# Latent and forgetting attention: value products one unit later, two token blocks at a time

## The chip, the cores and the metric

The kernel runs on 1 core of one Trainium2 chip. The metric is the device time of one launch in microseconds (us). Engines carry the names of the profile: PE is the tensor engine's matmul, PEld its weight load, DVE the vector engine, ACT the scalar engine, POOL GpSimd, SP the engine that issues most DMAs.

## The reference

The program computes one transformer block with two kinds of attention, and then two layers of a second kind with a convolution branch, a gated short convolution and latent attention. 512 tokens, width 1024, float32. What the change touches are two of the attentions. The first block's forgetting attention (8 heads of 64, after 16 meta tokens), for a block of 128 queries:

```python
sb = jnp.einsum('bqhd,bkhd->bhqk', q_blk, k) * scale
sb = sb + c_blk[..., None] - cum[:, :, None, :]
sb = jnp.where(k_pos[None, :] <= q_pos[:, None], sb, NEG_INF)
pb = jax.nn.softmax(sb, axis=-1).astype(v.dtype)
return jnp.einsum('bhqk,bkhd->bqhd', pb, v)
```

and the latent attention of the two later layers (8 heads, queries and keys of 64 + 32, values of 64), for a block of 128 queries:

```python
s = jnp.einsum("bqhd,bkhd->bhqk", qb, k) * scale
s = jnp.where(mask[None, None], s, -jnp.inf)
p = jax.nn.softmax(s, axis=-1).astype(v.dtype)
return jnp.einsum("bhqk,bkhd->bqhd", p, v)
```

Both are causal over the 512 tokens. The results go through output projections; everything else (norms, projections, feed-forward, convolutions, gates) is untouched.

## The kernel before

Activations are kept feature-major as [128, 512 tokens] tiles, each split in two float32r parts (hi, lo), so that a projection is three matmuls of 512 columns per 128 inputs (`mm3`, L117 to L122). A projection of one [128, 512] output is 24 such matmuls.

Both attentions work in units (i, b): pair of heads i (0 to 3), query block b (0 to 3), 16 units per attention; the latent attention runs once in each of two layers. A unit has two stages. `first` makes the scores of the two heads (tiles `s`: L687 and L690 in `fox`, L1531 to L1534 in `mla`), reduces them on DVE, takes exp on ACT into `L`, and scales `L` on DVE. `second`, one unit behind, transposes the b + 1 blocks of `L` of each head on PE into a PSUM tile (`pT`, L720 and L1554), copies that to SBUF on ACT (`ptile`, L722 and L1556), and multiplies it by the values into the PSUM tile `pv` (L726 and L1560): 2(b + 1) products with a stationary operand of 128 x 64, one head in each half of `pv`. At b = 3 the pair is closed: `fox` adds the meta tokens' product (L729) and splits `pv` (`mix_split`), `mla` gates it on DVE (`om`, L1564) and splits it. The scores and the transposes share three PSUM banks (`spp`), `pv` is a single bank (`pvp`), and the SBUF tiles for `pT` are two (`tp`).

Between the units stand fillers: projections (`pj`, `qn`, `qr`, `kb`, `q`), and in the later half of `fox` steps of the output projection (`y`). In `mla` they are spread by `pipeline` (L207), in `fox` by a table of steps. In `mla` the convolution's taps (L1217) run on DVE meanwhile.

The order on each engine isn't the order of the code: a scheduler places the instructions by priority (earlier code first) and by its own estimate of when their inputs are ready, so that matmuls of a filler stand between a unit's transposes and its value products. On the chip each engine runs its instructions in the order thus fixed.

Of the kernel before, what the change touches and what calls it, by code (L numbers as in the profile page):

```python
# [19 lines left out]
P = 128  # L20
# [18 lines left out]
class Cols:  # L39
    """[128, 8, 128] in two parts"""  # L40
# [8 lines left out]
class Kern:  # L49
    def __init__(self, ctx, tc, t, out):  # L50
        self.tc, self.nc, self.t, self.out = tc, tc.nc, t, out
        ep = lambda **k: ctx.enter_context(tc.tile_pool(**k))
        self.const = ep(name="const", bufs=1)
        self.wp = ep(name="wp", bufs=3)
        self.rowp = ep(name="rowp", bufs=3)
        self.ap = ep(name="ap", bufs=57)
        self.lp = ep(name="lp", bufs=3)
        self.tp = ep(name="tp", bufs=2)
        self.fp = ep(name="fp", bufs=4)
        self.qp = ep(name="qp", bufs=2)  # L60
        self.smp = ep(name="smp", bufs=32)
        self.mmp = ep(name="mmp", bufs=4, space=PSUM)
        self.spp = ep(name="spp", bufs=3, space=PSUM)
        self.pvp = ep(name="pvp", bufs=1, space=PSUM)
        self.dram = ep(name="dram", bufs=1, space=DRAM)
        self.n = 0
        self.bg = []
        self.rate = 0
        self.ahead = AHEAD
        self.lat_w = []  # L70
# [65 lines left out]
    def wrows(self, src):  # L136
        """a [128, 1024] row block, kept: hi and lo as two slabs each"""
# [15 lines left out]
    def wcols(self, w, c0, n, kt=KD):  # L153
        """[K, cols] -> hi, lo views [128, kt, n]"""
# [6 lines left out]
    def wkeep(self, w, c0):  # L161
        """[1024, 128] columns in slabs of their own"""
# [3 lines left out]
    def split(self, hi, lo, src, scale=None):  # L166
        """hi, lo <- src (SBUF or PSUM), optionally times a constant"""
# [8 lines left out]
    def rsqrt(self, v, n):  # L176
        """1 / sqrt(v), polished by a Newton step"""
# [19 lines left out]
    def bcast_row(self, dst, src, parts=P, eng=None):  # L197
        """DRAM row [n] -> all partitions"""
# [8 lines left out]
    def pipeline(self, first, second, fillers, lead=1):  # L207
        """units of two stages, the second one behind by some units; other work spread between them"""
        n, credit, fillers = len(first), 0.0, list(fillers)
        rate = len(fillers) / (n + lead)  # L210
        for i in range(n + lead):
            if i < n:
                first[i]()
            if i >= lead:
                second[i - lead]()
            credit += rate
# [7 lines left out]
    def setup(self):  # L224
        """everything small that the start needs, behind the first rows of x"""
# [43 lines left out]
    def squares(self, src, a, b, dve=False):  # L269
        """a, b <- row sums of squares of the halves of src [., 1024]"""  # L270
# [9 lines left out]
    def sumsq(self, rows):  # L280
        """[128, len(rows)] row sums of squares"""
# [38 lines left out]
    def warm(self, n):  # L320
        """keeps the tensor engine busy, so that its clock is up when the first products come"""
# [18 lines left out]
    def meta_rep(self):  # L340
        nc = self.nc
        mhi, mlo = self.mhl
        # replicated 8 times: [128, k, 8, 16]
# [10 lines left out]
    def swa_bias(self):  # L354
        """negated T5 bias with the window mask, per head: [meta | prev | cur] and, for the first block, [meta | cur]"""
# [41 lines left out]
    def q_load(self, i):  # L397
        """tile i holds heads i and i + 4"""
# [7 lines left out]
    def swa_first(self):  # L406
        """keys of the first half of the tokens, as soon as these are there"""
# [45 lines left out]
    def proj_v(self):  # L453
        """v_a, v_b and f, token-major"""
# [14 lines left out]
        # column halves: [v_a 128 | v_b 0:196] and [v_b 196:512 | f 8]  # L469
# [67 lines left out]
    def forget_sums(self):  # L537
        nc, ls = self.nc, self.ls
        # inclusive sums over the tokens, [head, token]
# [18 lines left out]
    def forget_rows(self, i):  # L558
        """the sums of two heads on all partitions"""
# [14 lines left out]
    def fox_k(self, i):  # L574
        """two steps, a half of the tokens each"""
# [17 lines left out]
    def probs(self, Lg, mn, den):  # L593
        """exp(min - Lg) in place, its sum in den"""
# [72 lines left out]
    def fox(self, mix, fillers):  # L667
        """pairs of heads one after another; fillers: a list per step"""
# [35 lines left out]
        def second(i, b):  # L704
            if b == 0:
                st[i, "pv"] = self.pvs()
            pv, Lt = st[i, "pv"], st.pop((i, b))
            n = (b + 1) * P
            tk = slice(b * P, n)
# [6 lines left out]
            pT = []  # L716
# [6 lines left out]
            for j in range(b + 1):  # L723
                for half in range(2):
                    h = 2 * i + half
                    nc.tensor.matmul(pv[64 * half:64 * half + 64, tk], lhsT=self.vb[j][:, h * 64:(h + 1) * 64],  # L726
                                     rhs=pT[half][:, j * P:(j + 1) * P], start=(b == 0), stop=False)
            if b == NB - 1:
                nc.tensor.matmul(pv, lhsT=self.vmF[:32, i * P:(i + 1) * P], rhs=pmT, start=False, stop=True)  # L729
# [3 lines left out]
        for s in range(len(u) + 1):  # L733
            if s < len(u):
                first(*u[s])
            if s:
                second(*u[s - 1])
            for f in fillers.get(s, ()):
                f()

    def tokmm(self, acts, wrow, kt, blocks, post, banks, tail=0):
        """token-major product as a list of steps: acts(k, b) -> (hi, lo) [128, 128 tokens]; wrow(k) -> hi, lo [2][128, 512];
        in the last `tail` row blocks the token blocks follow one another"""
# [42 lines left out]
    def add_rms(self, xs, g, ps):  # L786
        """x += rms_norm([p0 p1]) * g for some row tiles"""
# [10 lines left out]
    def to_feat(self, rows, hi, lo, c0, scale, bank, bias=None):  # L798
        """token-major row tiles -> feature-major hi, lo [k][:, c0:...], scaled and shifted per feature"""
# [208 lines left out]
    def layer_consts(self, l):  # L1008
        """per-channel vectors of a layer as columns"""
# [28 lines left out]
    def ada(self, l):  # L1038
        """queue the modulation of a layer: shift, 1 + scale as feature columns, gate as a row in DRAM"""
# [16 lines left out]
        def total(third):  # L1056
            """sums over the partitions, as a row in DRAM"""
# [31 lines left out]
    def colsum(self, ps, c0, src):  # L1089
        """ps[:, c0 + b] <- sums over the partitions of src[:, token block b]"""  # L1090
# [3 lines left out]
    def allsum(self, src):  # L1094
        """sums over the partitions [128, 512] in PSUM, the same in each partition"""
# [7 lines left out]
    def spread(self, cols, d):  # L1103
        """per-token columns [128, 4] -> [128, 512] in PSUM, the same in each partition; d: a tile to work in"""
# [33 lines left out]
    def layer_begin(self, l, u, banks):  # L1138
        """the part that needs the first half of the tokens only"""
# [7 lines left out]
    def layer(self, l, finish, xd):  # L1147
# [5 lines left out]
        # latents  # L1153
# [40 lines left out]
        # branch A input, in the shadow of the latents' norms  # L1194
# [28 lines left out]
        # values and keys  # L1223
# [31 lines left out]
        # attention and branch B  # L1255
# [4 lines left out]
        def uq(i):  # L1260
            """queries of two heads; the rotary rows of four heads come together: [odd 3 | odd 1 | even 0 | even 2] by 32"""
# [73 lines left out]
        # merge  # L1335
# [25 lines left out]
        # branch A: layer norm in the shadow of the gates  # L1361
# [53 lines left out]
        # merge of branch A, w_o  # L1415
# [76 lines left out]
    def nope(self, ps):  # L1492
        """two heads' rows -> the even head's tile [nope | rope | -] and the odd one's [0 | rope | nope]"""
# [9 lines left out]
    def rope_parts(self, ps, n):  # L1503
        """two tiles whose sum is the rotated rows"""
# [13 lines left out]
    def mla(self, Q, K, V, cg, oc, fillers):  # L1518
# [25 lines left out]
        def second(i, b):  # L1544
            n = (b + 1) * P
            tk = slice(b * P, n)
            if b == 0:
                st[i] = self.pvs()
            pv, Lt = st[i], st.pop((i, b))
            pT = []  # L1550
# [6 lines left out]
            for j in range(b + 1):  # L1557
                for half in range(2):
                    h = 2 * i + half
                    nc.tensor.matmul(pv[64 * half:64 * half + 64, tk], lhsT=V[j][:, h * 64:(h + 1) * 64],  # L1560
                                     rhs=pT[half][:, j * P:(j + 1) * P], start=(b == 0), stop=(b == NB - 1 and j == b))
            if b == NB - 1:
# [9 lines left out]
        self.pipeline([lambda a=a: first(*a) for a in u], [lambda a=a: second(*a) for a in u], fillers)  # L1572
# [90 lines left out]
```

## Time and profile before

| | |
|---|---|
| three runs | 1796.34 us median (1795.69 to 1797.44) |
| span of the profiled execution | 1792.5 us |
| PE busy | 1745.6 us (97%) |
| DVE busy | 1142.4 us (64%) |
| ACT busy | 690.2 us (39%) |
| forgetting attention (L687 to L729) | about 157 to 275 us |
| latent attention, first and second layer | about 800 to 955 us, about 1350 to 1505 us |

Busy time of PE counts each matmul from its start to a modelled end, and neighbours overlap, so 97% doesn't say that PE gets through its work as fast as it could. Better is the distance from one start to the next in the timeline. A float32 matmul such as the value product is two instructions on PE: 80 products on L726 and 160 on L1560 are 160 and 320 rows in the trace. The transposes and the float32r matmuls are one each.

### The profile page before, as it was taken

What the parts mean: (1) busy time and instruction counts of PE and PEld (TensorE: products, weight loads), DVE (VectorE), ACT (ScalarE), POOL (GpSimd) and SP (SyncE); (2) the same over time, 40 slices, a digit from 0 to 9 for tenths busy, and PEclk for the clock granted to TensorE, in tenths of its full rate; (3) what the DMA queues carried; (4) which work ended last, traced back from release to release, by engine and by line L of the source; (5) the groups of instructions that cost most, each with busy time, mean ns of one, the idle gap of its engine ahead of it and who ended that gap; (6) DMA issues with size and microseconds to landing.
All of it is one profiled execution on the core that took longest, in us unless ns stands there. A gap on an engine that the chain in (4) does not pass through costs nothing.

```text
span 1792.5 us, 22688 instructions
## 1 busy us (share of the span) xinstructions
PE 1745.6 (97%) x8652; PEld 1390.8 (78%) x8652; DVE 1142.4 (64%) x1963; ACT 690.2 (39%) x1294; POOL 53.4 (3%) x110
## 2 busy tenths in 40 slices
PE   6999999999999999999999999998999999999997
PEld 6877767877778879877777888877877777888876
DVE  5354457865833464579786584468479796774657
ACT  4454455333333455354432223333444443222430
POOL 2000001000000000100000000000100000000000
PEclk9999999999999999999999999999999999999999
DMA  4412136575833574422223333335232223333332
GB/s 130 117 48 82 48 95 223 193 246 161 277 121 130 189 245 139 101 77 68 64 71 94 94 94 94 94 105 174 83 84 68 64 71 86 100 85 106 87 101 94
DMA packets 263479, 206.39 MB, mean 115 GB/s; under 512 B 43924, under 2 KB 239800, under 8 KB 263370
## 3 DMA queue, kind: packets, MB, share of 16 engines
q1 hardware_dynamic: 263082, 204.67, 38.9%
q8 instruction: 68, 1.11, 0.3%
q14 instruction: 41, 0.34, 0.1%
q10 hardware_dynamic: 288, 0.26, 0.1%
HBM read 196.48 MB, written 8.43 MB: 114 GB/s over the span
## 4 chain that ended last, share of the span: by engine, by line
PE 88%; DVE 6%; ACT 2%; issue 2%; DMA 2%; POOL 0%; SPq 0%; DVEq 0%; ACTq 0%; POOLq 0%
PE pj L120 11%; PE pj L122 11%; PE pj L121 11%; PE gu L121 4%; PE gu L122 4%; PE gu L120 4%; PE y L751 3%; PE y L752 3%; PE y L753 3%; PE yt L122 2%; PE yt L121 2%; PE yt L120 2%; PE pv L1560 2%; PE lat L122 1%; PE lat L120 1%
## 5 line engine op out<-in xcount | busy, mean ns | idle before, releaser
L132 ACT CAST whi<-raw 128x1024 fp32r<-128x1024 f32 (+4 forms) x275 | 283.6, 1034 | 761.8 <-PE pj L121 377.9
L133 DVE TENSOR_TENSOR wlo<-raw,whi 128x1024 fp32r<-128x1024 f32 (+4 forms) x275 | 330.3, 1203 | 304.0 <-ACT whi L132 302.0
L120 PE MATMUL pj<-uh,whi 128*128 128x512 f32 x896 | 357.4, 399 | 0.0
L121 PE MATMUL pj<-ul,whi 128*128 128x512 f32 x896 | 355.2, 396 | 0.0
L122 PE MATMUL pj<-uh,wlo 128*128 128x512 f32 x896 | 355.2, 396 | 0.0
L122 PEld LDWEIGHTS pj<-uh,wlo 128*128 128x128 f32 x896 | 168.4, 188 | 40.3 <-issue 3.4
L120 PEld LDWEIGHTS pj<-uh,whi 128*128 128x128 f32 x896 | 168.8, 188 | 38.9 <-issue 3.1
L121 PEld LDWEIGHTS pj<-ul,whi 128*128 128x128 f32 x896 | 168.8, 188 | 38.3 <-issue 2.6
L1217 DVE SCALAR_TENSOR_TENSOR conv<-apad,lcol,conv 128x512 f32<-128x512 f32 x240 | 179.6, 748 | 4.8
L122 PE MATMUL gu<-h2h,wlo 128*128 128x512 f32 x320 | 126.2, 395 | 0.0
L121 PE MATMUL gu<-h2l,whi 128*128 128x512 f32 x320 | 126.2, 394 | 0.0
L120 PE MATMUL gu<-h2h,whi 128*128 128x512 f32 x320 | 126.2, 394 | 0.0
L120 PEld LDWEIGHTS gu<-h2h,whi 128*128 128x128 f32 x320 | 60.2, 188 | 14.5 <-issue 0.8
L122 PEld LDWEIGHTS gu<-h2h,wlo 128*128 128x128 f32 x320 | 60.1, 188 | 14.4 <-issue 0.5
L121 PEld LDWEIGHTS gu<-h2l,whi 128*128 128x128 f32 x320 | 60.1, 188 | 13.8
L1054 DVE SCALAR_TENSOR_TENSOR acc<-wada,cact,acc 128x1024 f32<-128x1024 f32 x48 | 61.6, 1283 | 12.1 <-DMA wada<-in_w_ada_dram 7.4
L751 PE MATMUL y<-whi,fh 128*128 128x512 f32 x152 | 60.4, 397 | 1.0 <-ACT whi L132 1.0
L752 PE MATMUL y<-wlo,fh 128*128 128x512 f32 x152 | 60.5, 398 | 0.8 <-DVE wlo L133 0.8
L753 PE MATMUL y<-whi,fl 128*128 128x512 f32 x152 | 60.2, 396 | 0.0
L752 PE MATMUL y<-wrl,mh 128*128 128x512 f32 x128 | 49.6, 398 | 0.0
L753 PE MATMUL y<-wrh,ml 128*128 128x512 f32 x128 | 49.1, 394 | 0.0
L751 PE MATMUL y<-wrh,mh 128*128 128x512 f32 x128 | 47.0, 395 | 0.0
(456 smaller groups left out, 3195.0 us busy)
## 6 DMA issues: line engine op xcount, KB each, us to landing
raw<-in_w_in_dram SPq DMA_DIRECT2D x131, 512.0 KB
wada<-in_w_ada_dram SPq DMA_DIRECT2D x48, 512.0 KB
raw<-in_w_gate_up_dram SPq DMA_DIRECT2D x44, 512.0 KB
raw<-in_w_down_dram SPq DMA_DIRECT2D x44, 512.0 KB
raw<-in_w_o_dram SPq DMA_DIRECT2D x16, 512.0 KB
raw<-in_w_out_dram SPq DMA_DIRECT2D x16, 256.0 KB
raw<-in_w_out_dram SPq DMA_DIRECT2D x8, 512.0 KB
xr<-x_d SPq DMA_DIRECT2D x8, 512.0 KB
```

The costliest lines, as they stand in the source:

```text
L120: mm(ps, lhsT=wh, rhs=xh, start=start, stop=False)
L121: mm(ps, lhsT=wh, rhs=xl, start=False, stop=False)
L122: mm(ps, lhsT=wl, rhs=xh, start=False, stop=stop)
L132: nc.scalar.copy(hi[:, :n], raw[:, :n])
L133: nc.vector.tensor_tensor(lo[:, :n], raw[:, :n], hi[:, :n].bitcast(F32), op=ALU.subtract)
L751: nc.tensor.matmul(o, lhsT=xh, rhs=w[0][c], start=(k == 0), stop=False)
L752: nc.tensor.matmul(o, lhsT=xh, rhs=w[1][c], start=False, stop=False)
L753: nc.tensor.matmul(o, lhsT=xl, rhs=w[0][c], start=False, stop=(k == kt - 1))
L1054: nc.vector.scalar_tensor_tensor(st[third], w, self.cact[:, k:k + 1], st[third], op0=ALU.mult, op1=ALU.add)
L1217: stt(conv[c], a, lc[:, c, j:j + 1], conv[c], op0=ALU.mult, op1=ALU.add)
L1560: nc.tensor.matmul(pv[64 * half:64 * half + 64, tk], lhsT=V[j][:, h * 64:(h + 1) * 64], rhs=pT[half][:, j * P:(j + 1) * P], start=(b == 0) ...
```

## The change

The value products move out of `second` into a new stage `third`, which stands one unit further back and runs at the odd query blocks alone: it does the products of blocks b - 1 and b together. `pipeline` gets a third list, and `fox` a loop that is one step longer. The tiles for transposed probabilities go from two to seven; the DMA scratch of the program is made smaller (1024), which makes room for them. No product, transpose, copy or DMA is added or removed. The diff, without the comments that it drops:

```diff
-        self.tp = ep(name="tp", bufs=2)
+        self.tp = ep(name="tp", bufs=7)
...
-    def pipeline(self, first, second, fillers, lead=1):
+    def pipeline(self, first, second, fillers, lead=1, third=()):
         n, credit, fillers = len(first), 0.0, list(fillers)
         rate = len(fillers) / (n + lead)
-        for i in range(n + lead):
+        for i in range(n + (2 * lead if third else lead)):
             if i < n:
                 first[i]()
-            if i >= lead:
+            if lead <= i < n + lead:
                 second[i - lead]()
+            if third and i >= 2 * lead:
+                third[i - 2 * lead]()
...
         def second(i, b):        # fox
-            if b == 0:
-                st[i, "pv"] = self.pvs()
-            pv, Lt = st[i, "pv"], st.pop((i, b))
+            Lt = st.pop((i, b))
...
-            pT = []
+            pT = st[i, "pT", b] = []
...
-            for j in range(b + 1):
-                for half in range(2):
-                    h = 2 * i + half
-                    nc.tensor.matmul(pv[64 * half:64 * half + 64, tk], lhsT=self.vb[j][:, h * 64:(h + 1) * 64],
-                                     rhs=pT[half][:, j * P:(j + 1) * P], start=(b == 0), stop=False)
             if b == NB - 1:
-                nc.tensor.matmul(pv, lhsT=self.vmF[:32, i * P:(i + 1) * P], rhs=pmT, start=False, stop=True)
+                st[i, "pmT"] = pmT
+
+        def third(i, b1):
+            if b1 == 1:
+                st[i, "pv"] = self.pvs()
+            pv = st[i, "pv"]
+            for b in (b1 - 1, b1):
+                pT = st.pop((i, "pT", b))
+                for j in range(b + 1):
+                    for half in range(2):
+                        h = 2 * i + half
+                        nc.tensor.matmul(pv[64 * half:64 * half + 64, b * P:(b + 1) * P], lhsT=self.vb[j][:, h * 64:(h + 1) * 64],
+                                         rhs=pT[half][:, j * P:(j + 1) * P], start=(b == 0), stop=False)
+            if b1 == NB - 1:
+                nc.tensor.matmul(pv, lhsT=self.vmF[:32, i * P:(i + 1) * P], rhs=st.pop((i, "pmT")), start=False, stop=True)
                 mix.append(self.mix_split(pv))
...
-        for s in range(len(u) + 1):
+        for s in range(len(u) + 2):
             if s < len(u):
                 first(*u[s])
-            if s:
+            if 0 < s <= len(u):
                 second(*u[s - 1])
+            if s > 1 and u[s - 2][1] % 2:
+                third(*u[s - 2])
...
         # mla: the same move, with om, its split and the pops at b1 == NB - 1 in third
+        after = lambda a: third(*a) if a[1] % 2 else None
+        self.pipeline([lambda a=a: first(*a) for a in u], [lambda a=a: second(*a) for a in u], fillers,
+                      third=[lambda a=a: after(a) for a in u])
...
-    nc = bacc.Bacc("TRN2", target_bir_lowering=False, num_devices=1)
+    nc = bacc.Bacc("TRN2", target_bir_lowering=False, num_devices=1, dynamic_dma_scratch_size=1024)
```

The order moves on PE inside the three attentions alone, apart from a few neighbouring `y` matmuls after the forgetting one; before the first attention, between them and behind them PE's order stays as it was. Two places:

PE, first layer's latent attention, pair 0, where the transposes (`pT`) of query block 2 stand. Before, from the second head's transposes on (L1554 are transposes, L1560 value products, L120 to L122 a filler's matmuls):

```order
L1554 MATMUL pT_1516_7359<-ident_7_101,L_1489_7222 128x128 x3
L1560 MATMUL pv_1476_7180<-pT_1515_7357,V_1440_7018 64x128
L120 MATMUL pj_1521_7377<-uh_1186_5738,whi_1519_7373 128x512
L121 MATMUL pj_1521_7377<-ul_1194_5746,whi_1519_7373 128x512
L122 MATMUL pj_1521_7377<-uh_1186_5738,wlo_1520_7374 128x512
L1560 MATMUL pv_1476_7180<-pT_1517_7363,V_1440_7018 64x128
L1560 MATMUL pv_1476_7180<-pT_1515_7357,V_1442_7027 64x128
L1560 MATMUL pv_1476_7180<-pT_1517_7363,V_1442_7027 64x128
L1560 MATMUL pv_1476_7180<-pT_1515_7357,V_1444_7036 64x128
L1560 MATMUL pv_1476_7180<-pT_1517_7363,V_1444_7036 64x128
L120 MATMUL pj_1521_7377<-uh_1187_5739,whi_1519_7373 128x512
```

The same place in the changed kernel, from the first head's transposes on (L1562 are the transposes, L1576 the value products):

```order
L1562 MATMUL pT_1513_7346<-ident_7_101,L_1488_7219 128x128 x3
L1576 MATMUL pv_1517_7358<-pT_1477_7182,V_1440_7018 64x128
L1576 MATMUL pv_1517_7358<-pT_1479_7186,V_1440_7018 64x128
L1576 MATMUL pv_1517_7358<-pT_1494_7242,V_1440_7018 64x128
L1576 MATMUL pv_1517_7358<-pT_1496_7247,V_1440_7018 64x128
L1576 MATMUL pv_1517_7358<-pT_1494_7242,V_1442_7027 64x128
L1562 MATMUL pT_1515_7352<-ident_7_101,L_1488_7219 128x128 x3
L1576 MATMUL pv_1517_7358<-pT_1496_7247,V_1442_7027 64x128
L120 MATMUL pj_1521_7371<-uh_1185_5737,whi_1519_7367 128x512
```

Before, the products are those of the block just transposed, and stand alone and in fives between filler matmuls; now they are those of blocks 0 and 1, and five of the six stand where the fillers between the two heads' transposes stood.

PE, one unit later, transposes of query block 3. Before:

```order
L1554 MATMUL pT_1527_7426<-ident_7_101,L_1509_7333 128x128 x4
L120 MATMUL pj_1537_7460<-uh_1185_5737,whi_1535_7456 128x512
L121 MATMUL pj_1537_7460<-ul_1193_5745,whi_1535_7456 128x512
L122 MATMUL pj_1537_7460<-uh_1185_5737,wlo_1536_7457 128x512
L1554 MATMUL pT_1529_7433<-ident_7_101,L_1509_7333 128x128 x4
L120 MATMUL pj_1537_7460<-uh_1186_5738,whi_1535_7456 128x512
L1560 MATMUL pv_1476_7180<-pT_1528_7431,V_1440_7018 64x128
L121 MATMUL pj_1537_7460<-ul_1194_5746,whi_1535_7456 128x512
L122 MATMUL pj_1537_7460<-uh_1186_5738,wlo_1536_7457 128x512
L1560 MATMUL pv_1476_7180<-pT_1530_7438,V_1440_7018 64x128
```

Now:

```order
L1562 MATMUL pT_1527_7420<-ident_7_101,L_1508_7326 128x128 x4
L120 MATMUL pj_1534_7440<-uh_1185_5737,whi_1532_7436 128x512
L1562 MATMUL pT_1529_7427<-ident_7_101,L_1508_7326 128x128 x4
L121 MATMUL pj_1534_7440<-ul_1193_5745,whi_1532_7436 128x512
L122 MATMUL pj_1534_7440<-uh_1185_5737,wlo_1533_7437 128x512
```

The products have left the place, and one filler matmul instead of three stands between the two heads' transposes.

## Rows read from the trace of the kernel before

**Rows 1.** The page, part 1: span, and PE's busy time, share, instructions.

```profile
span 1792.5 us, 22688 instructions
...
PE 1745.6 (97%) x8652; PEld 1390.8 (78%) x8652; DVE 1142.4 (64%) x1963; ACT 690.2 (39%) x1294; POOL 53.4 (3%) x110
```

**Rows 2.** The page, part 4: the chain that ended last, by engine.

```profile
PE 88%; DVE 6%; ACT 2%; issue 2%; DMA 2%; POOL 0%; SPq 0%; DVEq 0%; ACTq 0%; POOLq 0%
```

**Rows 3.** Attention stretches: length, then PE, PEld, DVE, ACT, POOL busy; PEclk; DMA.

```profile
157.00:275.00 118.00, 114.52 (x718) 81.94 (x717) 56.57 (x178) 57.50 (x143) 0.00 (x0) 0.99 0.28 81
800.00:955.00 155.00, 154.02 (x808) 114.97 (x807) 126.10 (x216) 64.91 (x141) 2.60 (x7) 1.00 0.27 72
1350.00:1505.00 155.00, 154.17 (x809) 115.23 (x808) 127.89 (x218) 65.50 (x141) 2.60 (x7) 1.00 0.26 68
```

**Rows 4.** Tile pv, its value products: duration min/median/max, first and last start.

```profile
L1560 PE MATMUL pv<-pT,V x320: 272/273/325, 803.8 to 1502.9; 128*64 128x128 f32 x160
...
L726 PE MATMUL pv<-pT,vb x160: 272/273/325, 173.0 to 271.5; 128*64 128x128 f32 x160
```

**Rows 5.** Timeline, forgetting attention, one run of value products: start, length, instruction.

```profile
178.99 0.40 PE L121 MATMUL q<-hnl,whi 128*128 128x512 f32 x1
...
179.31 0.65 PE L726 MATMUL pv<-pT,vb 128*64 128x128 f32 x6
...
179.89 0.50 PE L122 MATMUL q<-hnh,wlo 128*128 128x512 f32 x1
...
180.23 0.40 PE L120 MATMUL q<-hnh,whi 128*128 128x512 f32 x1
...
180.47 0.39 PE L121 MATMUL q<-hnl,whi 128*128 128x512 f32 x1
```

**Rows 6.** Timeline, PE, the last run of value products in the second layer.

```profile
1501.80 0.39 PE L120 MATMUL pj<-uh,whi 128*128 128x512 f32 x1
1502.12 1.09 PE L1560 MATMUL pv<-pT,V 128*64 128x128 f32 x14
1503.14 0.50 PE L121 MATMUL pj<-ul,whi 128*128 128x512 f32 x1
1503.48 0.39 PE L122 MATMUL pj<-uh,wlo 128*128 128x512 f32 x1
```

**Rows 7.** Waits of PEld: total us, times, longest us.

```profile
PEld pT L1554 <- ACT L L1536: 6.0, 13, 1.0
PEld pv L1560 <- ACT pT L1556: 6.0, 19, 0.5
PEld pT L1554 <- ACT pT L1556: 4.6, 15, 0.4
...
PEld pv L726 <- ACT pT L722: 2.7, 6, 0.7
```

**Rows 8.** Timeline at the second head's transposes of query block 3.

```profile
826.26 0.40 PE L122 MATMUL pj<-uh,wlo 128*128 128x512 f32 x1
...
826.68 0.37 ACT L1536 ACTIVATE L<-s,mn 128x128 f32<-128x128 f32 x1 [1.29 <-DVE mn L1535]
...
827.19 0.66 PE L1554 MATMUL pT<-ident,L 128*128 128x128 f32 x4 [0.54 <-ACT L L1536]
```

**Rows 9.** Timeline, PE, forgetting attention, units with no filler.

```profile
187.43 0.55 PE L720 MATMUL pT<-ident,L 128*128 128x128 f32 x3 [0.62 <-ACT pT L722]
...
189.23 0.87 PE L726 MATMUL pv<-pT,vb 128*64 128x128 f32 x10 [0.41 <-ACT pT L722]
```

**Rows 10.** Timeline, DVE, gate and split of the last pair's pv.

```profile
951.26 0.69 DVE L1564 SCALAR_TENSOR_TENSOR om<-pv,cg 128x512 f32<-128x512 f32 x1 [0.43 <-PE pv L1560]
...
952.64 0.69 DVE L171 TENSOR_TENSOR ocl<-om,och 128x512 fp32r<-128x512 f32 x1
```

**Rows 11.** Two stretches in the forgetting attention, columns as in rows 3.

```profile
198.00:201.40 3.40, 3.40 (x17) 3.40 (x16) 0.89 (x4) 0.88 (x4) 0.00 (x0) 0.51 0.03 5
201.40:204.80 3.40, 3.40 (x30) 3.08 (x28) 0.44 (x1) 0.39 (x1) 0.00 (x0) 1.00 0.00 0
```

More of the change, by code (lines that the diff above doesn't have):

```diff
@@ L704, in second @@
         def second(i, b):
-            if b == 0:
-                st[i, "pv"] = self.pvs()
-            pv, Lt = st[i, "pv"], st.pop((i, b))
+            Lt = st.pop((i, b))
             n = (b + 1) * P
-            tk = slice(b * P, n)
             if b == NB - 1:
@@ L1545, in second @@
             n = (b + 1) * P
[L1546 to L1550, printed above, removed]
+            Lt = st.pop((i, b))
+            pT = st[i, "pT", b] = []
             for half in range(2):
@@ L1556, in second, with third @@
                 nc.scalar.copy(pT[half][:, :n], tp[:, :n])
[L1557 to L1562, printed above, removed]
+        def third(i, b1):
+            if b1 == 1:
+                st[i] = self.pvs()
+            pv = st[i]
+            for b in (b1 - 1, b1):
+                pT = st.pop((i, "pT", b))
+                for j in range(b + 1):
+                    for half in range(2):
+                        h = 2 * i + half
+                        nc.tensor.matmul(pv[64 * half:64 * half + 64, b * P:(b + 1) * P], lhsT=V[j][:, h * 64:(h + 1) * 64],
+                                         rhs=pT[half][:, j * P:(j + 1) * P], start=(b == 0), stop=(b == NB - 1 and j == b))
+            if b1 == NB - 1:
                 om = self.lrow(F32, "om")[:, :S]
@@ L1571, in mla @@
         u = [(i, b) for i in range(4) for b in range(NB)]
-        self.pipeline([lambda a=a: first(*a) for a in u], [lambda a=a: second(*a) for a in u], fillers)
+        after = lambda a: third(*a) if a[1] % 2 else None
+        self.pipeline([lambda a=a: first(*a) for a in u], [lambda a=a: second(*a) for a in u], fillers,
+                      third=[lambda a=a: after(a) for a in u])
 @with_exitstack
```

## The prediction

> **What bounds the kernel now.** I read the page's busy times first: PE has work in flight for 97% of the span [rows 1]. The chain of waits, read next, agrees: 88% of it is PE [rows 2]. The change touches three stretches, so I went to these by windows. PE is busy for 114.5 of 118 us in the forgetting attention and for 154 of 155 us in each latent attention, while DVE has 57 and 126 to 128 us, ACT 57 and 65, and DMA a quarter [rows 3]. So the stretches end when PE is through its queue. The idle time that a better cover could give back is small: 3.5 us in the first stretch and 1 us in each of the others. If the change is worth more than that, it must make PE's own work shorter, though it removes no instruction.
>
> The timeline shows where that can come from. A filler matmul of 512 columns starts 0.23 to 0.24 us after the one ahead of it (the last two rows of [rows 5]). Around a run of value products it doesn't. From the filler ahead of a run to the second filler behind it 1.24 us pass for a run of 6 pieces [rows 5] and 1.68 us for one of 14 [rows 6]. One piece costs 0.055 us: the run of 6 lasts 0.58 us from its start to the next filler's start, that of 14 lasts 1.02 us, and (1.02 - 0.58)/8 is 0.055. Taking off two steps of 0.232 us and the pieces leaves 1.24 - 0.46 - 0.33 = 0.45 us and 1.68 - 0.46 - 0.77 = 0.45 us. So **each unbroken run costs 0.45 us beyond its pieces, however long it is**. It has three parts: the run starts 0.32 us after the filler ahead of it instead of 0.23, about 0.09 more; the filler behind starts 0.25 us later than the pieces alone would have it; and the next one comes 0.34 us after that instead of 0.23, 0.11 more. What is special about these products is the stationary operand of 128 x 64, where the neighbours have 128 x 128 [rows 4 to 6]. Read in the same way, the 51 runs with a 512-column matmul on both sides (first in rows 5, last in rows 6) have a median of 0.45 us, a lowest of 0.35, and a quarter over 0.54; those that are higher have a wait or another run right beside them.
>
> **The change part by part.** *Fewer runs.* By the order of PE's instructions the value products of the forgetting attention stand in 30 unbroken runs before and in 17 now, those of the two latent attentions in 59 and 26. The two places that the section on the change shows are typical: a run of one and a run of five for a unit before, and now a unit's slot either holds both blocks' products or none. The pieces stay 160 and 320 [rows 4] and cost what they cost. So 89 - 43 = 46 runs go: 46 x 0.45 = 20.7 us, of which 13 x 0.45 = 5.9 us lie in the forgetting attention and 33 x 0.45 = 14.9 us in the latent ones. Bounds from the same runs: 46 x 0.35 = 16 us and 46 x 0.54 = 25 us. I take 0.45, as 46 of the 89 runs are single products, most of them among fillers, and only 8 such are left. All of it is on PE's path, since PE has hardly an idle moment there [rows 3].
>
> That a switch costs something agrees with the Trainium skill, "TensorEngine Tiling (Array Packing)", Key Properties: a change of tiling mode drains the engine. But "TensorE: Matmul & The Clock Gate", Step-by-step, puts the drain at about 128 cycles; at 2.4 GHz two switches would be some 0.11 us a run (an estimate by that page) against the 0.45 us of the rows, and the sum would be 46 x 0.11, about 5 us.
>
> *Waits for the copies of pT.* Before, a value product waits for the copy of the tile just transposed: PEld lost 6.0 us to that in the latent attentions and 2.7 in the forgetting one [rows 7]. One unit later the copy is long done. Most of these waits are under the exit and entry of a run that I have counted, so I add nothing; the bound is another 3 us of gain.
>
> *Waits at the second head's transposes.* The scores and transposes share three banks, so the second head's transposes can have to wait until exp has read the first scores of the next unit. With the product gone the cover changes. At query block 2 it improves: five products (about 1.0 us with their run) stand where three fillers (0.70 us) stood. At query block 3 of pair 0 one filler is left of three. That place already waits before: the exp began at 826.68 and took 0.37 us, and PE, which had begun its last filler at 826.26, sat idle for 0.54 us until 827.19 [rows 8]. Two fillers less make it 2 x 0.232 = 0.46 us longer; it comes once in each layer, so 0.9 us. In the forgetting attention's units with no filler, PE waited 0.62 us before the second transposes and 0.41 us before a run of ten [rows 9]; five products now stand in the first gap and the second run has moved, so about 1.0 us comes back in the pair shown. These two cancel. What the new order holds of pairings that the old one never had (a transpose right behind a value product, 14 times) I bound by nothing and 0.45 us each, 0 to 6.3 us, and take 1 us: nearest is the exit of a run into a filler, which is counted already.
>
> *The rest.* More buffers take away a reason to wait and cost no time. The last pair's gate and split come later: `om` to the end of `ocl` took 951.26 to 953.33, 2.1 us [rows 10], and 24 filler matmuls (5.6 us) and nine of the consumer's own (2.1 us) stand between the last product and the first matmul that needs it, so it stays covered; if a busy DVE doubled it, 4.2 us would still be under 7.7. DVE, in order, is busy for 126 of 155 us; with PE some 7 us shorter it is 126 of 148, 85%, still not the bound. No DMA moves on its queue but for a few loads by a place or two, and DMA is busy for a quarter of these stretches.
>
> Sum: -20.7 + 1.0 = -19.7 us. Behind the attentions PE's order is unchanged, and PE was the bound there, so the gain is carried to the end. From the profiled span: 1792.5 - 19.7 = 1772.8 us. The median is 3.8 us over that span; 1796.3 - 19.7 = **1776.6 us**.
>
> **The rivals.** *The switches turn into waits.* With less PE work in a unit, the softmax's chain (reduce, exp, scale, copies) may end last in places where PE just covered it. For it: 23 waits of PE's weight loads on `L` or copies of `pT` already exist in such places, up to 1.0 us each [rows 7]. Against it: PE idles 1 us in 155 [rows 3], and the fillers are spread. If half of the gain comes back, 10 us, the time is 1786.
>
> *More than the runs.* If the 8.7 us of waits for the copies [rows 7] were only half inside the 0.45 us, and no new ones come, the gain is 20.7 + 4 = 25 us and the time 1771.5.
>
> *Only the entry goes.* Most of the fixed part could belong to the single products themselves and come along with them, so that only what a run pays at its entry is saved, 0.09 us each. For it: some single products stand beside a wait. Against it: runs of 6 and of 14 pieces have the same 0.45 us [rows 5, 6]. Then 46 x 0.09 = 4.1 us go, and the time is 1792. The drain of the Trainium skill ("TensorE: Matmul & The Clock Gate", Step-by-step) would give about the same, the 5 us above.
>
> *Slower.* The second head's transposes become the bound: bereft of the unit's own products and fillers, they wait in every unit for the exp of the next scores. There are 48 units; the wait of rows 8 with the two fillers gone is 0.54 + 0.46 = 1.0 us. At 0.43 us in every unit the gain of 20.7 us is gone; at 1.0 us the kernel is 27 us slower, 1824. Against it: in all but five of the 48 units (two in each latent attention, one in the other) as much PE work as before stands there, or more.
>
> **How the numbers follow.** Forecast 0.70 (1773 to 1782); waits take back half 0.13; more than the runs 0.09; only the entry 0.04; slower 0.04. The range goes from 1771 (the upper bound of 25 us) to 1786 (half comes back; also the lower bound, 16 us less 6 for the new pairings, 10 us): it leaves out the last two cases and the tails of the others. A change of 0.2%, 3.6 us, is about what a measurement of this kernel can tell from none. Faster by more: the first three and most of the fourth, 0.94; within: 0.03; slower: 0.03. One thing more moves by itself: PE's granted clock is 0.51 (its 1.2 GHz level) for 3.4 us after the forgetting attention's units with no filler [rows 11]; if that goes or comes once more it is 1.7 us, inside the range.
>
> **What would show it.** Right: the windows of the attentions shorter by about 6 and 7 us each, with the same counts of pieces; in the timeline runs of 10, 12, 18 or 28 pieces with 0.45 us around them; the waits of `pv` for ACT gone from PEld's list. Wrong: runs that cost 0.45 us still, but PE idle before L1562 or L719 (the changed kernel's transposes) for many units; or a longer run that loses more at its exit; or a stretch after the attentions that has grown by what they lost.

## The result and the profile after

The changed kernel takes **1766.2 us** (median; 1764.7 to 1767.3), the kernel before beside it 1796.0 us: 29.8 us less, a ratio of 0.9839 with an interval of 0.9827 to 0.9851. The forecast was 1776.6 us, its range 1771 to 1786. The sign and the main mechanism hold; the gain is 10 us larger than the sum said, and lies below the range.

The profiled execution of the changed kernel took 1767.2 us, of which the page shows 1765.4 as span, 27.1 us less than before [rows 1]. First two parts of its page, then the chain:

```profile
span 1765.4 us, 22661 instructions
...
PE 1721.6 (98%) x8652; PEld 1390.2 (79%) x8652; DVE 1140.2 (65%) x1963; ACT 690.8 (39%) x1294; POOL 52.8 (3%) x110
```

```profile
PE 88%; DVE 6%; issue 2%; ACT 2%; DMA 2%; POOL 1%; SPq 0%; DVEq 0%; ACTq 0%; POOLq 0%
```

The same 8652 matmuls keep PE busy for 24 us less, and PE still makes up 88% of the chain [rows 2]. The three attention stretches by windows, columns as in [rows 3]:

```profile
157.00:263.00 106.00, 104.18 (x716) 79.54 (x716) 56.47 (x178) 57.59 (x143) 0.00 (x0) 1.00 0.31 88
790.00:936.00 146.00, 145.55 (x788) 115.33 (x787) 124.46 (x215) 65.01 (x141) 2.34 (x7) 1.00 0.27 73
1333.00:1478.00 145.00, 144.57 (x784) 114.63 (x783) 125.00 (x214) 64.22 (x139) 2.33 (x7) 1.00 0.27 73
```

118 us have become about 106, and 155 about 146 and 145. PE's idle time in the first stretch fell from 3.48 us to 106.00 - 104.18 = 1.82; in the latent attentions there was little to lose, and half of it is gone. DVE works as much as before in a shorter stretch (85 and 86%) and hasn't become the bound.

A run of value products after the change, by the timeline of PE (start, length, instruction; L1562 are transposes, L1576 value products):

```profile
821.28 0.28 PE L1562 MATMUL pT<-ident,L 128*128 128x128 f32 x1
821.49 0.87 PE L1576 MATMUL pv<-pT,V 128*64 128x128 f32 x10
822.29 0.33 PE L1562 MATMUL pT<-ident,L 128*128 128x128 f32 x1
822.55 1.30 PE L1576 MATMUL pv<-pT,V 128*64 128x128 f32 x18
823.78 0.50 PE L120 MATMUL pj<-uh,whi 128*128 128x512 f32 x1
824.12 0.39 PE L121 MATMUL pj<-ul,whi 128*128 128x512 f32 x1
```

The run of 18 needs 1.23 us to the filler behind it: 18 x 0.055 = 0.99 and 0.24 at its exit; the next filler comes 0.34 us later. Those are the 0.25 and 0.34 of the run of 6 in [rows 5]. So the price of a run is still paid once, for three times the pieces.

The waits of PEld over the whole span that [rows 7] answer to (us in total, times, longest):

```profile
PEld pT L1562 <- ACT pT L1564: 3.8, 17, 0.3
PEld pT L1562 <- ACT L L1547: 3.4, 9, 0.5
PEld pv L1576 <- issue: 2.1, 10, 0.4
PEld pv L735 <- issue: 1.6, 9, 0.2
...
PEld pv L735 <- ACT pT L721: 0.2, 1, 0.2
```

The value products' waits for ACT (6.0 and 2.7 us before) are gone but for one of 0.2 us, and the transposes of the latent attentions wait less, not more: 7.2 us against 10.6.

**Where the 27.1 us are.** I took the start of every PE instruction from both traces, marked where each attention begins and ends by the same instructions, and summed for every run of value products what it costs beyond 0.055 us a piece and the undisturbed steps of its neighbours, as the prediction did for two of them:

| us | forgetting | latent 1 | latent 2 | sum |
|---|---|---|---|---|
| cost of the runs before (30, 29, 30 runs) | 15.8 | 13.3 | 13.9 | 43.0 |
| after (17, 13, 13) | 9.2 | 5.9 | 6.1 | 21.1 |
| **difference by runs** | -6.6 | -7.5 | -7.8 | **-21.9** |
| difference of the section | -12.2 | -8.1 | -9.0 | -29.3 |
| of this, half-clock stretch of [rows 11] gone | -1.7 | | | -1.7 |
| left over: waits and steps outside the runs | -3.9 | -0.6 | -1.2 | -5.7 |

Between the forgetting and the first latent attention 2.4 us are given back: about 1.4 of them in a half-clock stretch at 645.4 that before doesn't have, the rest in the first 20 us behind the forgetting attention, where a few `y` matmuls stand in another order and each execution has its half-clock stretch at another place. Everything else is -0.2: -29.3 + 2.4 - 0.2 = -27.1. The medians differ by 29.8, and the interval of the ratio is 27 to 31 us: in every run with both on record the time is about 1.8 us over the span, so the profiled execution of before (1792.5 us) was some 2 us shorter than its median, and that of the changed kernel 1.0 us longer.

### The profile page after: what moved, and what is told of

Its sections match the earlier page's. It is cut to its first block, busy times and chain, and to the rows that moved or that the text cites. A ratio compares the mean times of both kernels' runs of the same rounds, so it can differ in the third digit from the quotient of the medians.

```text
span 1765.4 us, 22661 instructions
## 1 busy us (share of the span) xinstructions
PE 1721.6 (98%) x8652; PEld 1390.2 (79%) x8652; DVE 1140.2 (65%) x1963; ACT 690.8 (39%) x1294; POOL 52.8 (3%) x110
## 4 chain that ended last, share of the span: by engine, by line
PE 88%; DVE 6%; issue 2%; ACT 2%; DMA 2%; POOL 1%; SPq 0%; DVEq 0%; ACTq 0%; POOLq 0%
PE pj L120 12%; PE pj L121 12%; PE pj L122 11%; PE gu L121 4%; PE gu L120 4%; PE gu L122 4%; PE y L763 4%; PE y L762 4%; PE y L764 4%; PE yt L122 2%; PE yt L121 2%; PE yt L120 2%; PE lat L122 1%; PE lat L120 1%; PE lat L121 1%
## 5 line engine op out<-in xcount | busy, mean ns | idle before, releaser
L120 PE MATMUL pj<-uh,whi 128*128 128x512 f32 x896 | 356.3, 398 | 0.0
L122 PE MATMUL pj<-uh,wlo 128*128 128x512 f32 x896 | 353.0, 394 | 0.0
L120 PEld LDWEIGHTS pj<-uh,whi 128*128 128x128 f32 x896 | 168.5, 188 | 40.1 <-issue 2.4
L122 PEld LDWEIGHTS pj<-uh,wlo 128*128 128x128 f32 x896 | 168.2, 188 | 38.5
L120 PE MATMUL gu<-h2h,whi 128*128 128x512 f32 x320 | 126.2, 394 | 0.0
L122 PE MATMUL gu<-h2h,wlo 128*128 128x512 f32 x320 | 126.0, 394 | 0.0
L122 PEld LDWEIGHTS gu<-h2h,wlo 128*128 128x128 f32 x320 | 60.0, 188 | 14.7 <-issue 0.3
L120 PEld LDWEIGHTS gu<-h2h,whi 128*128 128x128 f32 x320 | 60.1, 188 | 14.5 <-issue 0.8
```

The lines of the kernel that those rows point to most:

```text
L120: mm(ps, lhsT=wh, rhs=xh, start=start, stop=False)
L122: mm(ps, lhsT=wl, rhs=xh, start=False, stop=stop)
```

## The experiments

All are measured against the kernel before on the same chip. "Runs" are unbroken runs of value products; the cost of the runs is summed from each trace as above.

| kernel | runs | us | before | difference | ratio, interval | runs' cost, against 43.0 |
|---|---|---|---|---|---|---|
| e1_delay | 67 | 1775.3 | 1794.4 | -19.2 | 0.9890 (0.9876 to 0.9905) | 29.6: -13.4 |
| e2_join | 71 | 1782.8 | 1794.4 | -11.7 | 0.9932 (0.9916 to 0.9949) | 35.0: -8.0 |
| e3_bufs | 89 | 1794.3 | 1794.4 | -0.1 | 1.0000 (0.9990 to 1.0009) | 43.1: 0 |
| e4_wide | 86 | 1791.7 | 1794.4 | -2.7 | 0.9984 (0.9975 to 0.9994) | other pieces |
| e5_ahead | 31 | 1763.9 | 1796.1 | -32.2 | 0.9826 (0.9805 to 0.9848) | 13.2: -29.8 |
| e6_pair8 | 16 | 1756.1 | 1796.1 | -40.0 | 0.9782 (0.9765 to 0.9800) | 7.1: -35.9 |
| e6_pair9 | 16 | 1756.6 | 1796.1 | -39.5 | 0.9786 (0.9768 to 0.9804) | 7.0: -36.0 |
| e7_fox | 76 | 1783.8 | 1795.4 | -11.6 | 0.9940 (0.9926 to 0.9953) | 36.4: -6.6 |
| e8_mla | 56 | 1776.7 | 1795.4 | -18.6 | 0.9895 (0.9881 to 0.9909) | 27.8: -15.2 |
| e9_foxdelay | 83 | 1788.7 | 1795.4 | -6.7 | 0.9964 (0.9951 to 0.9977) | 38.7: -4.3 |

Fewer runs went with a gain in each of the eight kernels that have them and leave the product's shape alone, and in each the gain is 2.4 to 5.8 us more than the runs explain; for the change itself it is 7.9 (29.8 against 21.9).

**e1_delay: the delay without the joining.** Against the changed kernel, in both attentions:

```diff
-            for b in (b1 - 1, b1):
+            for b in (b1,):
...
-            if s > 1 and u[s - 2][1] % 2:
+            if s > 1:
```

> The changed kernel, but the third stage runs at every query block and does that block's products alone: one unit later, not two blocks together. By the order of PE's instructions the value products stand in 67 unbroken runs (24 + 43), against 89 before and 43 with the change. Theory 'runs' (each unbroken run costs 0.48 us, the mean of the 89 runs before): 22 x 0.48 = 10.6 us less than before by the runs; and, if the part of the change's gain that its runs don't explain (about 8 us) comes from the delay, another 5 to 8 us, so 15 to 19 us less. Rival 'copies' (the gain is that no product waits for the copy of its pT any more, however the products are grouped): 27 to 30 us less, as with the change.

19.2 us less: a little over the theory, far under the 27 to 30 us that it would be if the copies' waits were everything. The delay alone leaves 67 runs of 89, since a block's products then stand together more often.

**e2_join: the joining without the delay.** Both blocks' products stand right behind the second block's transposes:

```diff
-            if s > 1 and u[s - 2][1] % 2:
-                third(*u[s - 2])
+                if u[s - 1][1] % 2:
+                    third(*u[s - 1])
```

> Two token blocks together without the delay: the products of blocks b - 1 and b follow directly on the transposes of block b, with the changed kernel's seven buffers. 71 unbroken runs (28 + 43). Theory 'runs': 18 x 0.48 = 8.6 us less than before, and no more, since products wait for their copies as before. Rival 'copies': within 2 us of before.

11.7 us less, where a value near nothing would have said that only the waits count. Here the copies of the odd block are as fresh as before, and it still gains what its 18 fewer runs give and 3 to 4 us more. Neither half makes the gain alone.

**e3_bufs: the kernel before with seven buffers and the small scratch.**

```diff
-        self.tp = ep(name="tp", bufs=2)
+        self.tp = ep(name="tp", bufs=7)
...
-    nc = bacc.Bacc("TRN2", target_bir_lowering=False, num_devices=1)
+    nc = bacc.Bacc("TRN2", target_bir_lowering=False, num_devices=1, dynamic_dma_scratch_size=1024)
```

> The kernel before with seven buffers for pT in place of two and the smaller DMA scratch, nothing else. 89 runs as before. Theory 'runs': no change, within 2 us. Rival 'buffers' (the gain beyond the runs comes from the copies no longer waiting for a free buffer): 4 to 8 us less.

No change to 0.1%. The buffers are what the later stage needs, and worth nothing by themselves. This run showed something else: with the same order on PE its profiled execution has more half-clock stretches than the one of before, and its span is 2.9 us longer. Windows, columns as in [rows 3]:

```profile
199.00:202.40 3.40, 3.40 (x17) 3.40 (x16) 0.89 (x4) 0.76 (x3) 0.00 (x0) 0.50 0.02 5
656.40:659.80 3.40, 3.40 (x8) 2.72 (x9) 2.44 (x2) 1.04 (x1) 0.00 (x0) 0.50 0.67 198
```

The first is the stretch of [rows 11], which both have; the second stands between the attentions, where before ran at full clock and the changed kernel has one, too (at 645.4). So which of these 3.4 us stretches an execution gets is not a matter of the order alone; one cost 1.4 to 1.7 us, by the same instructions in a trace with and one without it. They are a part of the scatter between executions: the shortest and the longest of the kernel before that were measured beside e5_ahead, 1790.7 and 1798.3 us, have mean granted clocks of 0.995 and 0.992.

**e4_wide: the kernel before, with both heads' values as stationary operand, 128 columns instead of 64.**

```diff
-                    nc.tensor.matmul(pv[64 * half:64 * half + 64, tk], lhsT=V[j][:, h * 64:(h + 1) * 64],
+                    nc.tensor.matmul(pv[:, tk], lhsT=V[j][:, i * P:(i + 1) * P],
```

> The kernel before, but each value product of the forgetting and latent attentions takes both heads' values as its stationary operand (128 x 128 instead of 128 x 64) and writes all of pv, so the two heads' results are added up: the output of the attentions isn't the reference's. 86 runs, but no change of the operand's width at their ends. A product of this shape takes 0.216 us instead of 0.11 (two pieces at 0.108, as the meta products of the windowed attention), so 240 products cost 25 us more. Theory 'runs', in the form that the change between 128 and 64 columns is what costs 0.48 us: -89 x 0.48 + 25 = 17 to 18 us less than before. If the fixed cost belongs to any run of value products, or to waits: 25 us more.

2.7 us less: neither number. The timeline shows why, here at a run of 6 (L1560 are the value products):

```profile
924.89 0.39 PE L121 MATMUL pj<-ul,whi 128*128 128x512 f32 x1
925.12 0.92 PE L1560 MATMUL pv<-pT,V 128*128 128x128 f32 x6
925.80 0.48 PE L122 MATMUL pj<-uh,wlo 128*128 128x512 f32 x1
926.12 0.40 PE L120 MATMUL pj<-uh,whi 128*128 128x512 f32 x1
```

The entry is 0.23 us, an ordinary step, instead of the 0.32 of [rows 5]. The run takes 0.68 us to the next filler; one of 8 takes 0.91, so a piece costs 0.115 us instead of 0.055, and the six pieces alone fill the 0.68. So **at full width the entry's 0.09 us and the exit's 0.25 us are gone**. The step from that filler to the next is still 0.32 us, so the last part of the 0.45, about 0.1 us, isn't due to the width. Counted as in the table above with 0.11 to 0.115 us a piece, the 86 runs cost 9 to 12 us, not 43.

The pieces spend what the runs gain: 480 of them at 0.055 to 0.06 us more are 26 to 29 us. I had reckoned with 25 us for them, but with all of the runs' 43 us as gain. From filler to second filler it is 1.23 us against the 1.24 of [rows 5]: at 6 pieces the two are even. A run of 14 loses, with 2.02 us (1497.26 to 1499.28) against the 1.68 of [rows 6]; a run of 2 gains, 0.77 us against 1.12 at the same place, e4_wide first and then before:

```profile
825.31 0.48 PE L120 MATMUL pj<-uh,whi 128*128 128x512 f32 x1
825.63 0.38 PE L1560 MATMUL pv<-pT,V 128*128 128x128 f32 x2
825.77 0.47 PE L121 MATMUL pj<-ul,whi 128*128 128x512 f32 x1
826.08 0.39 PE L122 MATMUL pj<-uh,wlo 128*128 128x512 f32 x1
```

```profile
827.60 0.48 PE L120 MATMUL pj<-uh,whi 128*128 128x512 f32 x1
828.02 0.43 PE L1560 MATMUL pv<-pT,V 128*64 128x128 f32 x2
828.38 0.50 PE L121 MATMUL pj<-ul,whi 128*128 128x512 f32 x1
828.72 0.39 PE L122 MATMUL pj<-uh,wlo 128*128 128x512 f32 x1
```

With the width, the products' alternation between the two halves of `pv` goes as well; no run tells these two apart.

**e5_ahead: the changed kernel with `third` written ahead of `second`**, so that the products come right behind the scores, with no transposes among them:

```diff
+            if s > 1 and u[s - 2][1] % 2:
+                third(*u[s - 2])
             if 0 < s <= len(u):
                 second(*u[s - 1])
-            if s > 1 and u[s - 2][1] % 2:
-                third(*u[s - 2])
```

> The changed kernel with the third stage written ahead of the second in each step, so that the scheduler places a step's value products in one piece ahead of its transposes. 31 unbroken runs (15 + 16) against 43 with the change. Theory 'runs' (0.48 us each, and the delay's share of about 5 us kept): 58 x 0.48 + 5 = 33 us less than before, 6 us less than with the change. Rival 'cover' (the products between the two heads' transposes were what hid the wait for a free bank): the 12 runs are saved, but the 14 places where products stood between transposes wait 0.3 to 0.5 us each, so the same as the change or up to 2 us slower.

32.2 us less, 2.4 more than the change; in the profiled spans 31.3 against 27.1. That is near the theory's 33, but the intervals of the two ratios overlap, so the times alone don't decide. By the traces both were half right: 31 runs cost 13.2 us, 7.9 less than in the changed kernel, but outside the runs only 1.5 us are saved where the change saved 5.2, probably as the products no longer stand between the two heads' transposes, which no run shows by itself.

**e6_pair8 and e6_pair9: the products of all four blocks once per pair**, `third` ahead of `second`, with eight buffers and with nine:

```diff
-            for b in (b1 - 1, b1):
+            for b in range(NB):
...
-            if s > 1 and u[s - 2][1] % 2:
+            if s > 1 and u[s - 2][1] == NB - 1:
```

> As the kernel with the third stage ahead, but that stage runs once for a pair of heads and does all four token blocks together, with eight buffers for pT. 16 unbroken runs (8 + 8). Theory 'runs': 73 x 0.48 + 5 = 40 us less than before, about 1755 us. Rival 'buffers': eight tiles are exactly one pair's, so the next pair's first copy waits until the products of this one are through; eight such places a few us each would take back 10 to 20 us.

> The same with nine buffers for pT. Theory 'runs': the same as with eight within 2 us, about 1755 us. Rival 'buffers': several us faster than with eight.

1756.1 and 1756.6 us: as forecast, alike, and 10 us under the changed kernel. Eight buffers are enough. One of the runs of 40 pieces (e6_pair8, PE):

```profile
857.40 0.23 PE L1545 MATMUL s<-mkb,idb 128*128 128x128 bf16 x1
857.56 2.40 PE L1576 MATMUL pv<-pT,V 128*64 128x128 f32 x40
859.89 0.44 PE L1562 MATMUL pT<-ident,L 128*128 128x128 f32 x2
860.09 0.47 PE L120 MATMUL pj<-uh,whi 128*128 128x512 f32 x1
```

2.33 us for 40 pieces are 2.20 and 0.13 at the exit. Entered behind the bf16 mask matmul and left into transposes, a run costs 0.30 us (1.21 us for the four of a latent attention) instead of 0.45.

**e7_fox and e8_mla: the change in one kind of attention alone; e9_foxdelay: the delay of e1_delay in the forgetting attention alone.** These ask where the 10 us lie that the prediction missed. In the attention that is left alone, `third` follows `second` at once, block by block, which is the order of before (here in `mla`, for e7_fox and e9_foxdelay):

```diff
-        after = lambda a: third(*a) if a[1] % 2 else None
-        self.pipeline([lambda a=a: first(*a) for a in u], [lambda a=a: second(*a) for a in u], fillers,
-                      third=[lambda a=a: after(a) for a in u])
+        def both(i, b):
+            second(i, b)
+            third(i, b)
+
+        self.pipeline([lambda a=a: first(*a) for a in u], [lambda a=a: both(*a) for a in u], fillers)
```

> The change in the forgetting attention alone; both latent attentions keep the order of the kernel before (seven buffers and the smaller scratch stay). 72 runs of value products instead of 89. Theory (what the prediction missed lies in the forgetting attention: there the one-unit delay also takes away waits of PE for copies and score banks, and the stretch at half clock behind the units with no filler): runs 6.6 us less by the two profiles, 3.9 us of waits and up to 1.7 us of clock: 10 to 13 us faster than before. Rival (the miss is spread, or is how one execution differs from the next): the runs' 6 to 7 us only.

> The change in both latent attentions alone; the forgetting attention keeps the order of the kernel before. 56 runs of value products instead of 89. Theory: 33 runs less, 15.3 us by the two profiles, and 1.8 us of waits: 16 to 18 us faster than before; with the gain of the other half-change about 29 us, the whole gain. Rival (the miss is spread over all three attentions in proportion to the runs): 29.8 us x 33/46 = 21 us faster.

> In the forgetting attention alone, and the delay alone: the products stand one unit later, each block's by themselves; nothing else moves. 24 runs there instead of 30. Theory (the delay takes the waits away, whether or not products are joined): runs 4.4 us less, waits 2.9 us less, up to 1.7 us of clock: 7 to 9 us faster than before, and the joining adds 3 to 4 us to that. Rival (only the number of runs counts): 2.7 us (six runs at 0.45 us) to 4.4 us.

By its trace e7_fox has 76 runs, 17 + 59, not the 72 of the expectation; the prices there don't use that number. It gains 11.6 us, inside the theory's 10 to 13 and well over the 6 to 7 of the runs. e8_mla gains 18.6, a little over the theory's 16 to 18; its interval, 16 to 21 us, doesn't exclude the rival's 21. Together they make 30.2, the whole gain: the two parts add up. So of the 10 us, 11.6 - 5.9 = 5.7 lie in the forgetting attention and 18.6 - 14.9 = 3.7 in the two latent ones. e9_foxdelay gains 6.7 us, just under the theory's 7 to 9; its interval, 4.1 to 8.8, takes in the rival's 4.4, so this run alone doesn't decide between them. Windows of e7_fox (the changed attention) and of e8_mla (the first latent one; and the place of [rows 11]):

```profile
156.00:263.50 107.50, 105.74 (x715) 81.00 (x714) 56.45 (x178) 57.56 (x143) 0.00 (x0) 0.98 0.30 87
```

```profile
797.00:944.00 147.00, 146.54 (x794) 116.41 (x793) 126.19 (x217) 65.81 (x145) 2.33 (x7) 1.00 0.28 73
```

```profile
198.00:201.40 3.40, 3.40 (x30) 3.08 (x29) 1.33 (x5) 0.69 (x3) 0.00 (x0) 1.00 0.02 5
```

In e7_fox's profile the stretch at half clock came at 167.8 instead of 198, so the clock gives it nothing; its section is 10.5 us shorter, 6.7 by runs and 3.8 by the rest. That 3.8 is the same as the changed kernel's 3.9, which speaks against scatter. e8_mla has before's order in the forgetting attention and yet full clock at 198. Of the three profiles with that order (before, e3_bufs, e8_mla) two have the stretch of [rows 11] there; of the seven with the products one unit later none has it there. So it isn't a matter of the order alone, and so few executions can't say whether the change makes it rarer: its 1.7 us can't be put to the change's credit.

## Why the prediction was right, and where it was wrong

**Fewer runs: right.** 46 runs fewer were to give 20.7 us and gave 21.9. The mean cost was 0.48 us, the median, which I took, 0.45; the difference of the two, 89 x 0.03 or some 3 us, I put down to those runs that had a wait in them. The 43 runs that are left cost 0.49 us each, so that the sum came so near is in part luck: both sides were taken too low. That it is runs and not pieces is what e1_delay, e2_join, e5_ahead and the two e6 kernels show: with the same 480 pieces, 67, 71, 31 and 16 runs cost 29.6, 35.0, 13.2 and 7 us. The rival that only the entry goes, with 4.1 us, is out by a factor of five. The estimate by the drain of the Trainium skill ("TensorE: Matmul & The Clock Gate", Step-by-step), about 5 us for the whole change, is out by a factor of four here.

**Waits for the copies of `pT`: the first step that failed.** I put them at nothing, under the runs' exits, with a bound of 3 us, though the rows were there: 2.7 us of weight loads of `pv` and 0.41 us of idle PE [rows 7, 9]. In the forgetting attention, where units without a filler leave nothing to cover a copy, taking them off was worth more, and I had let it cancel against a loss that never came. Beyond its runs that attention gained 3.9 us (3.8 in e7_fox; 2.9 in e9_foxdelay, so most of it belongs to the delay). PE's idle time names 1.7 of it, and most of that is waits for copies of `pT`: 1.9 us before and 0.4 us after. They are these, first before (L726 value products, L720 transposes, L687 scores), then after:

```profile
PE pv L726 <- ACT pT L722: 1.0, 2, 0.5
PE pT L720 <- ACT pT L722: 0.6, 1, 0.6
PE s L687 <- ACT pT L722: 0.3, 1, 0.3
```

```profile
PE pTm L712 <- ACT pT L721: 0.4, 1, 0.4
```

The second head's transposes of [rows 9], timeline of PE after the change (L719 transposes, L735 value products, L712 those for the meta tokens):

```profile
185.21 0.87 PE L735 MATMUL pv<-pT,vb 128*64 128x128 f32 x10
186.01 0.55 PE L719 MATMUL pT<-ident,L 128*128 128x128 f32 x3
...
187.66 0.61 PE L712 MATMUL pTm<-ident,pm 128*32 128x128 f32 x4 [0.40 <-ACT pT L721]
```

Five products (ten pieces) now stand where PE waited 0.62 us, as forecast, and a part of the wait has moved on to the meta tokens' transposes (0.40). The rest of the 3.9 us, about 2.2, is spread over many short steps that PE counts as busy; its cause stays open.

**Query block 3's transposes: wrong in sign.** Two fillers less were to make the wait of [rows 8] 0.46 us longer in each layer. It became shorter: the second head's four transposes start 0.57 us after the filler, of which 0.31 is the ordinary step of a filler behind transposes (814.95 to 815.26 in the same timeline), so they wait 0.26 us. By the same count it was 0.93 - 0.23 = 0.70 us before [rows 8]. PE, then DVE after the change:

```profile
813.54 0.23 PE L1545 MATMUL s<-mkb,idb 128*128 128x128 bf16 x1
813.61 0.61 PE L1562 MATMUL pT<-ident,L 128*128 128x128 f32 x4
813.97 0.48 PE L120 MATMUL pj<-uh,whi 128*128 128x512 f32 x1
814.54 0.65 PE L1562 MATMUL pT<-ident,L 128*128 128x128 f32 x4
```

```profile
813.04 0.69 DVE L1325 TENSOR_TENSOR cv<-cv,pj 128x512 f32<-128x512 f32 x1
813.65 0.48 DVE L1546 TENSOR_REDUCE mn<-s 128x1 f32<-128x128 f32 x2
```

And DVE at the same place of the kernel before:

```profile
824.79 0.69 DVE L1314 TENSOR_TENSOR cv<-cv,pj 128x512 f32<-128x512 f32 x1 [0.71 <-PE pj L122]
825.43 0.96 DVE L133 TENSOR_TENSOR wlo<-raw,whi 128x768 fp32r<-128x768 f32 x1
826.30 0.48 DVE L1535 TENSOR_REDUCE mn<-s 128x1 f32<-128x128 f32 x2
```

The exp waits for DVE's reduce, and before, a weight split of 0.96 us stood ahead of that reduce in DVE's queue. It now stands elsewhere, so the reduce begins 0.11 us after the last score matmul instead of 1.0. I had counted the cover on PE and taken the releaser's time as given. The wait in the second layer shrank likewise, from 0.64 to 0.20 us.

**New pairings: a cost of 1 us that wasn't there.** A run between transposes costs 0.40 us, less than one between fillers, and 0.50 where a single transpose parts it from the next run. In the latent attentions the rest is a gain of 1.8 us, not a loss of 1.9; beyond the wait at query block 3, which gives some 0.9 of it, its cause isn't shown.

**The sum.** I had -20.7 + 1.0 = -19.7; the trace has -21.9 for the runs, -5.7 beside them, -1.7 for a half-clock stretch and +2.4 between the attentions, 1.4 of it another such stretch, and the medians 2.7 more than the spans. So the steps that failed are what I set beside the runs: +1.0 us, where the trace has -5.7. *More than the runs*, at 0.09, was the nearest rival: its mechanism (waits outside the 0.45 us) is right for the forgetting attention, and even its 1771.5 was too high. *The switches turn into waits* and *slower* failed, since PE waits less for ACT than before. (The 23 waits that I counted for the first of these are 28 by [rows 7], 13 for `L` and 15 for copies.)

**The range** ended at 1771 because I set it to the runs' upper bound of 25 us alone. The 3 us of copies and the 1.7 of the clock, both named in the text, belonged on top: 25 + 3 + 1.7 = 29.7 us, or 1766.6.

**The rest held.** The end of the latent attention stayed covered, DVE didn't become the bound, and the buffers cost nothing (e3_bufs).

## What to carry to other kernels

Where few narrow matmuls stand among wide ones, count the unbroken runs, not the instructions: with 0.45 us a run, grouping them paid here until nothing was left to group (16 runs here, e6_pair8, another 10 us), and the buffers that this takes cost nothing as long as they fit. Widening the stationary operand takes away most of a run's fixed cost but makes each piece dearer, so it paid here for runs below some six pieces only. And before calling a wait longer or shorter, look at what its releaser has queued ahead; bounds with different causes are added, not set side by side.

## What the runs showed of the hardware

- A piece of a float32 product of 128 columns took 0.055 us with a stationary operand of 64 columns and 0.106 to 0.115 us with one of 128 (e4_wide, runs of 14 and of 6 to 8). The weight loads differ, but less, by the tile views of the changed kernel and of e4_wide (duration min/median/max):

```profile
L1576 PEld LDWEIGHTS pv<-pT,V x320: 132/137/137, 805.5 to 1486.0; 128*64 128x64 f32 x160
```

```profile
L1560 PEld LDWEIGHTS pv<-pT,V x320: 186/192/248, 802.6 to 1498.8; 128*128 128x128 f32 x160
```

- The price of a run depends on its neighbours: 0.45 us between 512-column matmuls, 0.40 between transposes, 0.30 from the bf16 mask matmul into transposes. At full width about 0.1 us of the 0.45 was left (e4_wide).
- Stretches of 3.4 us at a granted clock of 0.50 (the 1.2 GHz level) come at different places in executions of the same order, and cost 1.4 to 1.7 us each. Ahead of the one at 645.4 in the changed kernel PE had been busy for 1.62 of the 3.4 us before it; the one of [rows 11] follows the units without fillers.
